# Down projection of a SwiGLU FFN: sixteen of its 22 blocks by seven products of halves

## The chip, the cores and the metric

The kernel runs on one core of one Trainium2 chip. The metric is the device time of one execution in microseconds, the median of several runs. The profile beside it comes from one further execution, taken by the hardware profiler. Engines are PE (TensorE), DVE (VectorE), ACT (ScalarE), POOL (GpSimd) and SP (SyncE, which here only issues DMAs).

## What is computed

One decoder layer on 512 tokens of width 1024 in float32: a norm, a projection, two attention-like head groups, an output projection with residual, and then the part that matters here, a dense FFN with `D_FF = 2816` and a last norm.

```python
def swiglu(x, w_gate, w_up, w_down):
    return (jax.nn.silu(x @ w_gate) * (x @ w_up)) @ w_down
...
        h = h + swiglu(rms_norm(h, norm_ffn[l]), w_gate[l], w_up[l], w_down[l])
    return rms_norm(h, norm_final)
```

The down projection is the last product, (512 x 2816) by (2816 x 1024), added to the residual.

## The kernel before

Every float32 matmul is made of three: each operand is split into a high part `hi` (a rounded copy, ACT, L144) and a low part `lo` (the rest, a subtraction on DVE, L146) by `split`, and `mm3` (L162 to L165) issues hi x hi, hi x lo and lo x hi into one PSUM bank. A matmul has a stationary operand of 128x128 and a moving one of 256 or 512 columns.

**FFN, gate and up** (L1174 to L1207). Eleven passes `q` make 256 of the 2816 hidden columns each. A pass forms gate and up from seven products of half-depth operands (`prod`, 24 matmuls of 256 columns each): the activations' sums and splits (`A11`, `S1`, ...) are made once and kept, in `gin` and `kB` among others, while `weight_side` loads four weight quarters, forms their sums (two by DMAs on POOL's queue that add into a tile, two on DVE) and splits seven operands `B11, B21, T2, T1, T3, B22, T4` into the rotating buffers `whi` and `wlo`, two of each. The results `hid` lie as [hidden column in block, token], four blocks of 128 to a `b8` tile and the last two in a `t4` tile.

**Down projection** (`accumulate`, called at L1211 with 22 blocks). Eight PSUM banks hold the whole output, four token tiles `t` by two halves `f` of the 1024 columns. For each pair of blocks, `weights` loads 256 rows of `w_down` (1 MB, SP's queue, three buffers `wraw`) and splits them into `whi`, `wlo` (in two halves); `jit` splits the hidden blocks into a ring in an `L` buffer. Then 48 matmuls of 128x512 follow, so 11 x 48 = 528 in all. The last four blocks run token tile by token tile, and behind each token tile come the residual, the final norm and the store.

Instructions stand in each engine's queue in an order that a scheduler chose when the program was built, by its own estimates and by priorities (`tc.high_priority`); on the chip every engine works down its queue in that order. Buffers are few: four of 16 KB a partition (`L`, one of them held by the residual `x2`), three `wraw`, two `whi`, two `wlo`, four `t4`. The PSUM banks are `s`, `pj`, `ra` (two each), `o` and `rb`.

Of the kernel before, what the change touches and what calls it, by code (L numbers as in the profile page):

```python
# [46 lines left out]
def hybrid_layer(ctx: ExitStack, tc: tile.TileContext, x, positions, norm_mix, w_in, mu_shift, w0, w2, a0, a2,  # L47
# [90 lines left out]


    def split(src, hi, lo, pool=False, lo_pool=False):  # L140
        if pool:
            POOL.tensor_copy(hi, src)
        else:
            ACT.activation(hi, src, AF.Copy)  # L144
        pool = pool or lo_pool
        (POOL if pool else DVE).tensor_sub(lo, src, hi.bitcast(F32))  # L146
# [1116 lines left out]
```

## Time and profile before

| | |
|---|---|
| median of 3 runs | 769.43 us (767.77 to 770.11) |
| the profiled execution's own time | 770.73 us |
| its span, first to last instruction | 769.0 us |
| first matmul of the down projection | 642.45 us |
| last matmul of the down projection | 761.93 us |
| mean granted PE clock over the span | 0.984 |

Times inside the span count from its first instruction. The span lies 1.7 us under the profiled execution's own time, which lies 1.3 us above the median. Busy time of an engine says how full its queue is, not that the others wait for it: that is read from the waits, and from the chain of work that ended last.

### The profile page before, as it was taken

The numbers are of one execution on the slowest core, as the hardware profiler recorded it, in microseconds if no ns is written. First come the engines' busy times: TensorE is split into PE (matmuls) and PEld (weight loads), VectorE is DVE, ScalarE is ACT, GpSimd is POOL, SyncE is SP. The second block draws the span as 40 slices with busy tenths as digits, with TensorE's granted clock in tenths as the row PEclk, the third lists the DMA queues.
The fourth block names the chain that finished last, engine by engine and source line by source line (L and its number), as shares of the span: only waits on it lengthen the run. The fifth ranks groups of instructions, "written<-read, shape, count | busy, mean of one in ns | idle before, by whom it ended". The sixth has DMA issues, their size and how long they took to land.

```text
span 769.0 us, 14989 instructions
## 1 busy us (share of the span) xinstructions
PE 738.6 (96%) x6093; PEld 648.1 (84%) x6093; DVE 543.3 (71%) x1052; ACT 381.5 (50%) x652; POOL 160.0 (21%) x258
## 2 busy tenths in 40 slices
PE   8999999998889999999996899999999999999996
PEld 7867888898877878867786899999999998888885
DVE  5488689789768987875659497888695994333235
ACT  7398643224277776676447344444443552233224
POOL 3210054058345542442001102020202000000000
PEclk9999999999989999999998999999999999999998
DMA  7722543100051000321218569696768444322102
GB/s 247 223 82 84 164 110 110 55 2 2 3 219 30 3 1 3 85 83 56 83 55 192 110 176 203 161 223 151 161 159 221 112 153 147 110 68 97 55 1 110
DMA packets 69243, 82.83 MB, mean 108 GB/s; under 512 B 4868, under 2 KB 62806, under 8 KB 69174
## 3 DMA queue, kind: packets, MB, share of 16 engines
q1 hardware_dynamic: 57558, 70.34, 28.5%
q0 software_dynamic: 11616, 11.54, 9.9%
q8 instruction: 48, 0.79, 0.4%
q14 instruction: 21, 0.17, 0.1%
HBM read 79.77 MB, written 2.10 MB: 106 GB/s over the span
## 4 chain that ended last, share of the span: by engine, by line
PE 74%; DVE 15%; DMA 6%; issue 2%; ACT 1%; POOL 0%; SPq 0%; DVEq 0%; POOLq 0%; ACTq 0%
PE ps_ra L165 7%; PE ps_ra L164 7%; PE ps_ra L163 6%; PE ps_pj L165 6%; PE ps_pj L163 6%; PE ps_pj L164 6%; PE ps_s L165 4%; PE ps_s L163 4%; PE ps_s L164 4%; PE ps_o L1001 3%; DVE wlo L146 3%; PE ps_pj L993 2%; DMA L<-in_w_up_dram 2%; DMA wraw<-in_w_up_dram 2%; DMA L<-in_w_gate_dram 2%
## 5 line engine op out<-in xcount | busy, mean ns | idle before, releaser
L144 ACT ACTIVATE whi<-wraw 128x1024 fp32r<-128x1024 f32 (+1 forms) x79 | 78.5, 1033 | 33.2 <-PE ps_s L165 8.2
L146 DVE TENSOR_TENSOR wlo<-wraw,whi 128x1024 fp32r<-128x1024 f32 (+1 forms) x62 | 77.7, 1284 | 14.9 <-ACT whi L144 11.3
L146 DVE TENSOR_TENSOR L<-b,L 128x512 fp32r<-128x512 f32 x24 | 16.2, 691 | 57.1 <-PE ps_rb L164 55.1
L990 POOL TENSOR_SCALAR whi<-whi,m,gates 128x128 f32<-128x128 f32 (+3 forms) x64 | 42.5, 679 | 36.9 <-DVE m L988 28.7
L144 ACT ACTIVATE L<-b 128x512 fp32r<-128x512 f32 x24 | 14.9, 632 | 70.0 <-PE ps_rb L164 65.1
L164 PE MATMUL ps_ra<-wlo,L 128*128 128x256 f32 (+1 forms) x140 | 47.6, 340 | 0.2 <-DVE wlo L146 0.2
L163 PE MATMUL ps_ra<-whi,L 128*128 128x256 f32 (+1 forms) x140 | 47.4, 340 | 0.2 <-ACT L L144 0.2
L165 PE MATMUL ps_ra<-whi,L 128*128 128x256 f32 (+1 forms) x140 | 47.0, 337 | 0.0
L165 PE MATMUL ps_pj<-whi,L 128*128 128x256 f32 (+1 forms) x140 | 46.3, 332 | 0.0
L164 PE MATMUL ps_pj<-wlo,L 128*128 128x256 f32 (+1 forms) x140 | 46.3, 331 | 0.0
L163 PE MATMUL ps_pj<-whi,L 128*128 128x256 f32 (+1 forms) x140 | 45.9, 332 | 0.0
L164 PE MATMUL ps_ra<-L,whi 128*128 128x256 f32 (+2 forms) x128 | 44.3, 346 | 1.0 <-DVE L L146 1.0
L163 PE MATMUL ps_ra<-L,whi 128*128 128x256 f32 (+2 forms) x128 | 44.1, 345 | 0.9 <-ACT L L144 0.9
L165 PE MATMUL ps_ra<-L,wlo 128*128 128x512 f32 (+2 forms) x120 | 41.2, 343 | 0.0
L987 ACT ACTIVATE whi<-whi,m 128x128 f32<-128x128 f32 (+3 forms) x64 | 35.4, 554 | 9.3 <-DVE m L986 8.1
L165 PE MATMUL ps_pj<-L,wlo 128*128 128x512 f32 (+1 forms) x112 | 38.8, 346 | 0.1
L163 PE MATMUL ps_pj<-L,whi 128*128 128x512 f32 (+1 forms) x104 | 36.3, 349 | 0.2 <-ACT whi L144 0.2
L164 PE MATMUL ps_pj<-L,whi 128*128 128x512 f32 (+1 forms) x104 | 35.9, 346 | 0.0
L986 DVE CUSTOM_DVE_ANT_0 whi<-ps_s,negb 128x128 f32<-128x128 f32 (+3 forms) x64 | 29.3, 484 | 5.9 <-PE ps_pj L993 2.5
L1137 POOL DMA_DIRECT2D t<-in_w_up_dram x6 | 7.9, 1322 | 115.1 <-DVE whi L146 50.4
L163 PEld LDWEIGHTS ps_ra<-whi,L 128*128 128x128 f32 x140 | 27.6, 197 | 3.1 <-ACT L L144 0.6
L164 PEld LDWEIGHTS ps_ra<-wlo,L 128*128 128x128 f32 x140 | 27.5, 196 | 3.0 <-DVE wlo L146 0.5
(627 smaller groups left out, 2462.4 us busy)
## 6 DMA issues: line engine op xcount, KB each, us to landing
wraw<-in_w_gate_dram SPq DMA_DIRECT2D x22, 512.0 KB
wraw<-in_w_down_dram SPq DMA_DIRECT2D x11, 1024.0 KB
wraw<-in_w_in_dram SPq DMA_DIRECT2D x9, 1024.0 KB
t<-in_w_up_dram POOLq DMA_DIRECT2D x12, 512.0 KB, 7.4
wraw<-in_w_up_dram SPq DMA_DIRECT2D x11, 512.0 KB
L<-in_w_up_dram POOLq DMA_DIRECT2D x10, 512.0 KB, 8.9
wraw<-in_w_out_dram SPq DMA_DIRECT2D x4, 1024.0 KB
wraw<-in_w_in_dram SPq DMA_DIRECT2D x6, 512.0 KB
```

Of the source, the lines that this page charges most:

```text
L144: ACT.activation(hi, src, AF.Copy)
L146: (POOL if pool else DVE).tensor_sub(lo, src, hi.bitcast(F32))
L163: PE.matmul(o, lh, rh, start=start, stop=False)
L164: PE.matmul(o, lh, rl, start=False, stop=False)
L165: PE.matmul(o, ll, rh, start=False, stop=stop)
L986: DVE.tensor_tensor_reduce(pr[:, i], pS[:, i], negb[:, S - n:S], scale=-1.0, scalar=3e38, op0=OP.add, op1=OP.min, accum_out=m[:, i, 0:1])
L987: ACT.activation(pr[:, i], pr[:, i], AF.Exp, scale=-1.0, bias=m[:, i, 0:1], accum_out=m[:, i, 1:2])
L990: POOL.tensor_scalar(pr[:, i], pr[:, i], m[:, i, 2:3], gv[:, 1 + b0 + i, h:h + 1], op0=OP.mult, op1=OP.mult)
L993: PE.transpose(pT[:, j], prr[:, x, j * 128:j * 128 + 128], ident)
L1001: PE.matmul(po[q, 2 * g:2 * g + 2], vtok[:, j % (t + 1), b0 + j // (t + 1), g], pTs[:, par, j], start=False, stop=g == 1 and bs[-1] == 1 a ...
L1137: POOL.dma_start(t1, quarter(w_up, 0), accum_op=OP.add)
```

## The change

The blocks 0 to 7 and 12 to 19 of the hidden dimension are paired into two groups, blocks 0 to 3 with 12 to 15 and 4 to 7 with 16 to 19 (`GROUPS`). A group is a product of a 2 x 2 arrangement of halves, tokens (0 to 255, 256 to 511) by blocks (first four, second four), with a 2 x 2 arrangement of weights, blocks by columns (0 to 511, 512 to 1023), and is formed from seven products `m1` to `m7` instead of eight. A product (`multiply`) is four blocks by two token tiles by `mm3`, 24 matmuls of 128x512 in two PSUM banks. The sums of activations are made in place on DVE (L1263, L1265, L1274, L1300), those of weights on DVE (L1269, L1271, L1298) and by DMAs on POOL's queue (L1270). `a_side` splits 1024 columns of activations into the rotating `whi` and `wlo`, `b_side` splits 2048 columns of weights, in two halves, into an `L` buffer, behind the last split of the FFN's weights (`issue_after`). First come `m1, m5, m6, m7` of the first group and of the second, then their sums go into the residual `x2` (L1277 to L1291), then `m2, m4, m3` of both groups. The remaining six blocks (`PLAIN`) run through `accumulate` as before, in the banks of `m2`, `m3`, `m4` and one more pair.

```diff
-    def accumulate(hi, lo, w, blocks, ahead=None):
-
-        banks = [ps(o) for o in ORDER]
+    def accumulate(hi, lo, w, blocks, ahead=None, rows=None, banks=None, empty=None):
+
+
+        rows = rows or [n * 256 for n in range(blocks // 2)]
+        banks = banks or [ps(o) for o in ORDER]
+        empty = empty or banks
...
+    GROUPS = ((0, 12), (4, 16))
+    PLAIN = (8, 9, 10, 11, 20, 21)
...
+    def a_side(v):
+        o = operand(("whi", "wlo")[turn2[0] % 2])
+        turn2[0] += 1
+        split(v, *o)
+        return o
+
+    def b_side(v):
+        o = st([128, 2, 4, 512], "L", dtype=F32R)
+        with tc.high_priority(), tc.issue_after(ends[0]), tc.issue_after(ends[1]):
+            for h in (slice(0, 2), slice(2, 4)):
+                split(v[h.start // 2] if type(v) is list else v[:, h], o[:, 0, h], o[:, 1, h])
+        return o[:, 0], o[:, 1]
...
+    def multiply(banks, a, b, first, last=False):
+        for i in range(4):
+            for t in range(2):
+                tl = slice(t * 128, t * 128 + 128)
+                mm3(banks[t], a[0][:, i, tl], a[1][:, i, tl], b[0][:, i], b[1][:, i], first and i == 0, last and i == 3)
...
+    m1, m5, m6, m7 = ([ps(o) for o in two] for two in (("o", "rb"), ("pj", "pj"), ("ra", "ra"), ("s", "s")))
+    t2s = []
+    for n, (a, b) in enumerate(GROUPS):
+        one, two = halves[n]
+        a11, a21, a12, a22 = (h[:, :, x] for h in (one, two) for x in (left, right))
+        first, last = n == 0, n == 1
+        t1, t2 = block4(a, 0, "wraw"), block4(b, 1, ("gin", "kB")[n])
+        t3 = st([128, 4, 512], "wraw") if first else None
+        t3 = [t3[:, 2 * i:2 * i + 2] if first else st([128, 2, 512], "t4") for i in range(2)]
+        for i in range(2):
+            nc.sync.dma_start(t3[i], down(a, 1)[:, 2 * i:2 * i + 2])
+        t2s.append(t2)
+        DVE.tensor_sub(a21, a22, a21)
+        multiply(m1, a_side(a11), b_side(t1), first, last)
+        DVE.tensor_add(a11, a21, a11)
+        with tc.high_priority():
+            for i in range(2):
+                h = slice(2 * i, 2 * i + 2)
+                DVE.tensor_add(t1[:, h], t1[:, h], t3[i])
+                POOL.dma_start(t3[i], down(b, 1)[:, h], accum_op=OP.add)
+            DVE.tensor_add(t2, t2, t1)
+        multiply(m5, a_side(a21), b_side(t1), first, last)
+        multiply(m6, a_side(a11), b_side(t2), first, last)
+        DVE.tensor_sub(a21, a11, a22)
+        multiply(m7, a_side(a21), b_side(t3), first, last)
+    u, w, v = (st([128, 2, 512], tag) for tag in ("t4", "t4", "t4"))
+    with tc.high_priority():
...
+        for t in range(2):
+            DVE.tensor_add(u[:, t], m1[t], u[:, t])
+            DVE.tensor_add(x2[:, t, lo_], m1[t], x2[:, t, lo_])
...
+    m2, m4, m3, rest = ([ps(o) for o in two] for two in (("o", "rb"), ("pj", "pj"), ("ra", "ra"), ("s", "s")))
+    for n, (a, b) in enumerate(GROUPS):
+        one, two = halves[n]
+        a11, a12, a22 = one[:, :, left], two[:, :, left], two[:, :, right]
+        b21, b22 = block4(b, 0, "wraw"), block4(b, 1, "wraw")
+        multiply(m2, a_side(a12), b_side(b21), n == 0)
+        DVE.tensor_add(t2s[n], t2s[n], b21)
+        multiply(m4, a_side(a22), b_side(t2s[n]), n == 0)
+        DVE.tensor_sub(a12, a12, a11)
+        multiply(m3, a_side(a12), b_side(b22), n == 0)
...
+    held = [m2[0], m3[0], m2[1], m3[1], m4[0], rest[0], m4[1], rest[1]]
+    for t, banks in accumulate(*jit(lambda k: hid[PLAIN[k]]), w_down, 6, None, [PLAIN[k] * 128 for k in (0, 2, 4)], held, rest):
```

Three places in the built order show where the new work stands. DVE's queue at the end of the FFN, before: `whi_7057` is the FFN's last operand (T4), the L1187 to L1207 rows evacuate the last products, and `wraw_7263` and `wraw_7323` are the first two loads of `w_down`.

```order
L146 TENSOR_TENSOR whi_7057<-t4_7028,whi_7057 128x1024
L1194 TENSOR_TENSOR t2_7062<-ps_ra_7143,t2_7060 128x512
L1197 TENSOR_TENSOR t2_7060<-ps_s_7169,t2_7060 128x512
L1198 TENSOR_TENSOR lora_7063<-ps_s_7169,t2_7062 128x512
L146 TENSOR_TENSOR wlo_7266<-wraw_7263,whi_7265 128x1024 x2
L1201 TENSOR_TENSOR t2_7062<-ps_pj_7196,t2_7062 128x512
L1202 SCALAR_TENSOR_TENSOR t4_7024<-t2_7062,t2_7061 128x2x256
L1205 TENSOR_TENSOR t2_7060<-ps_ra_7223,t2_7060 128x512
L146 TENSOR_TENSOR wlo_7326<-wraw_7323,whi_7325 128x1024 x2
L1207 SCALAR_TENSOR_TENSOR t4_7024<-lora_7063,t2_7060 128x2x256
```

The same queue after the change, from a little behind the same split on: `wraw_7259` is t1 and `gin_7261` t2 of the first group, `wlo_7267`, `whi_7305` are the activations of `m1` and `m5`, `L_7308` the weights of `m5`, and `b8_4804` the hidden blocks 0 to 3.

```order
L1269 TENSOR_TENSOR wraw_7259<-wraw_7259,wraw_7263 128x1024
L142 TENSOR_TENSOR wlo_7267<-b8_4804,wlo_7267 128x1024
L1199 TENSOR_TENSOR t2_7060<-ps_s_7169,t2_7060 128x512
L1200 TENSOR_TENSOR lora_7063<-ps_s_7169,t2_7062 128x512
L1269 TENSOR_TENSOR wraw_7259<-wraw_7259,wraw_7263 128x1024
L142 TENSOR_TENSOR whi_7305<-b8_4804,whi_7305 128x1024
L142 TENSOR_TENSOR L_7308<-wraw_7259,L_7308 128x1024
L1265 TENSOR_TENSOR b8_4804<-b8_4804 128x4x256
L1203 TENSOR_TENSOR t2_7062<-ps_pj_7196,t2_7062 128x512
L1271 TENSOR_TENSOR gin_7261<-gin_7261,wraw_7259 128x2048
L1207 TENSOR_TENSOR t2_7060<-ps_ra_7223,t2_7060 128x512
L142 TENSOR_TENSOR L_7308<-wraw_7259,L_7308 128x1024
```

The evacuations of the last FFN products, which stood nearly alone, now stand among sums and splits of the down projection. Further down DVE's queue before, within the down projection, there are two kinds of rows only, in turn:

```order
L146 TENSOR_TENSOR wlo_7386<-wraw_7383,whi_7385 128x1024 x2
L146 TENSOR_TENSOR L_7254<-b8_5220,L_7254 128x512 x2
L146 TENSOR_TENSOR wlo_7446<-wraw_7443,whi_7445 128x1024 x2
L146 TENSOR_TENSOR L_7254<-b8_5671,L_7254 128x512 x2
L146 TENSOR_TENSOR wlo_7506<-wraw_7503,whi_7505 128x1024 x2
```

After the change, DVE's queue at the point where the banks of `m1` (`ps_o_7251`, `ps_rb_7252`) are read out for the sums, so that `m2` can take them:

```order
L142 TENSOR_TENSOR L_7517<-t4_7407,L_7517 128x1024
L142 TENSOR_TENSOR L_7579<-wraw_7572,L_7579 128x1024 x2
L142 TENSOR_TENSOR whi_7609<-b8_6122,whi_7609 128x1024
L1298 TENSOR_TENSOR kB_7404<-kB_7404,wraw_7674 128x2048
L1283 TENSOR_TENSOR t4_7546<-ps_o_7251,t4_7546 128x512
L1284 TENSOR_TENSOR L_4391<-ps_o_7251,L_4391 128x512
L142 TENSOR_TENSOR L_7612<-gin_7261,L_7612 128x1024 x2
L1283 TENSOR_TENSOR t4_7546<-ps_rb_7252,t4_7546 128x512
L1284 TENSOR_TENSOR L_4391<-ps_rb_7252,L_4391 128x512
```

The readout of `o` stands behind the splits of `m2` and `m4`'s activations and behind a sum of 2048 columns. PE's queue before, where one bank of the down projection follows the other:

```order
L164 MATMUL ps_s_7256<-wlo_7446,L_7254 128x512
L165 MATMUL ps_s_7256<-whi_7445,L_7254 128x512
L163 MATMUL ps_s_7256<-whi_7445,L_7254 128x512
L164 MATMUL ps_s_7256<-wlo_7446,L_7254 128x512
L165 MATMUL ps_s_7256<-whi_7445,L_7254 128x512
```

PE's queue after, from the end of `m5` (`pj`) of the first group to the body of `m6` (`ra`); `s` is `m7`, and `o`, `rb` with `L_7414`, `wlo_7411` are `m1` of the second group:

```order
L160 MATMUL ps_pj_7254<-L_7308,whi_7305 128x512
L161 MATMUL ps_pj_7254<-L_7308,whi_7305 128x512
L162 MATMUL ps_pj_7254<-L_7308,whi_7305 128x512
L160 MATMUL ps_s_7257<-L_7373,whi_7370 128x512
L160 MATMUL ps_s_7258<-L_7373,whi_7370 128x512
L160 MATMUL ps_o_7251<-L_7414,wlo_7411 128x512
L160 MATMUL ps_rb_7252<-L_7414,wlo_7411 128x512
L161 MATMUL ps_ra_7255<-L_7340,wlo_7337 128x512
L162 MATMUL ps_ra_7255<-L_7340,wlo_7337 128x512
```

Two hi x hi matmuls each of `m7` and of the next group's `m1` stand ahead of the body of `m6`; in the order before, a bank's matmuls follow each other without any of a later product between them.

## Rows read from the trace of the kernel before

**Rows 1.** The page's part 1: busy time, share of the span and number of instructions of each engine.

```profile
PE 738.6 (96%) x6093; PEld 648.1 (84%) x6093; DVE 543.3 (71%) x1052; ACT 381.5 (50%) x652; POOL 160.0 (21%) x258
```

**Rows 2.** Stretches of 20 us: the stretch, its length, then busy us (and instructions) of PE, PEld, DVE, ACT and POOL, the granted PE clock, the share of the DMA engines and GB/s. The first lies in the FFN, the second in the down projection.

```profile
620.00:640.00 20.00, 20.00 (x170) 20.00 (x169) 16.44 (x19) 8.55 (x10) 0.00 (x0) 1.00 0.32 107
...
680.00:700.00 20.00, 20.00 (x90) 16.57 (x89) 6.80 (x8) 6.33 (x8) 0.00 (x0) 1.00 0.30 105
```

**Rows 3.** The chain that ended last, from 590 us on: start, us, what. The first matmul of the down projection, its last one, and the step behind it.

```profile
642.45 0.23 PE ps_s L163
...
761.93 0.24 PE ps_rb L165
762.19 0.70 DVE L L1230
```

**Rows 4.** Who waited for whom on PE between 440 and 769 us: us in total, times, longest. It is the only wait.

```profile
PE ps_ra L165 <- DVE wlo L146: 0.7, 1, 0.7
```

**Rows 5.** DVE in order of time within the down projection: start, us, line, what, count, and in brackets the idle time before it with its releaser.

```profile
653.15 1.37 DVE L146 TENSOR_TENSOR L<-b,L 128x512 fp32r<-128x512 f32 x2 [6.61 <-PE ps_rb L164]
654.78 2.36 DVE L146 TENSOR_TENSOR wlo<-wraw,whi 128x1024 fp32r<-128x1024 f32 x2 [0.26 <-ACT whi L144]
664.03 1.37 DVE L146 TENSOR_TENSOR L<-b,L 128x512 fp32r<-128x512 f32 x2 [6.89 <-PE ps_rb L164]
```

**Rows 6.** DVE in order of time in the FFN, four instructions in a row without idle time between them.

```profile
618.36 0.68 DVE L1197 TENSOR_TENSOR t<-ps_ra,t 128x512 f32<-128x512 f32 x1
618.96 0.68 DVE L1198 TENSOR_TENSOR smask<-ps_ra,t 128x512 f32<-128x512 f32 x1
619.56 1.21 DVE L146 TENSOR_TENSOR whi<-wraw,whi 128x1024 fp32r<-128x1024 f32 x1
620.69 1.21 DVE L146 TENSOR_TENSOR wlo<-wraw,wlo 128x1024 fp32r<-128x1024 f32 x1
```

**Rows 7.** ACT in order of time at the same place, two splits in a row, and the split of the last FFN operand.

```profile
617.38 1.05 ACT L144 ACTIVATE whi<-wraw 128x1024 fp32r<-128x1024 f32 x1
618.32 1.05 ACT L144 ACTIVATE wlo<-wraw 128x1024 fp32r<-128x1024 f32 x1
...
631.13 1.06 ACT L144 ACTIVATE whi<-t 128x1024 fp32r<-128x1024 f32 x1 [1.02 <-PE ps_pj L165]
```

**Rows 8.** DVE in order of time in the last pass of the FFN (q = 10): evacuations of products, and the last FFN weights' split (632.23).

```profile
631.08 0.69 DVE L1191 TENSOR_TENSOR t<-ps_pj,t 128x512 f32<-128x512 f32 x1 [0.48 <-PE ps_pj L165]
632.23 1.23 DVE L146 TENSOR_TENSOR whi<-t,whi 128x1024 fp32r<-128x1024 f32 x1 [0.47 <-ACT whi L144]
633.89 0.69 DVE L1194 TENSOR_TENSOR t<-ps_ra,t 128x512 f32<-128x512 f32 x1 [0.44 <-PE ps_ra L165]
636.76 0.69 DVE L1197 TENSOR_TENSOR t<-ps_s,t 128x512 f32<-128x512 f32 x1 [2.17 <-PE ps_s L165]
...
640.23 0.68 DVE L1201 TENSOR_TENSOR t<-ps_pj,t 128x512 f32<-128x512 f32 x1
...
642.49 0.69 DVE L1205 TENSOR_TENSOR t<-ps_ra,t 128x512 f32<-128x512 f32 x1 [0.85 <-PE ps_ra L165]
```

**Rows 9.** DVE in order of time earlier in the FFN: an idle stretch, and the four splits of the first down-projection blocks.

```profile
593.65 1.23 DVE L1141 TENSOR_TENSOR L<-L,wraw 128x1024 f32<-128x1024 f32 x1 [6.53 <-DMA L<-in_w_up_dram]
...
615.94 2.49 DVE L146 TENSOR_TENSOR L<-b,L 128x512 fp32r<-128x512 f32 x4
```

**Rows 10.** SP's queue in order of time, and stretches of 2 us behind its first issue (columns as in rows 2).

```profile
613.53 27.18 SPq L78 DMA_DIRECT2D wraw<-in_w_down_dram  x4
...
614.00:616.00 2.00, 2.00 (x19) 2.00 (x18) 1.90 (x4) 0.72 (x2) 0.00 (x0) 1.00 0.55 150
616.00:618.00 2.00, 2.00 (x19) 2.00 (x19) 2.00 (x4) 2.00 (x4) 0.00 (x0) 1.00 0.91 375
```

**Rows 11.** DMA issues: tile, queue, count, KB each, median us from issue to landing; then one such transfer as a piece of the chain that ended last.

```profile
t<-in_w_up_dram POOLq DMA_DIRECT2D x12, 512.0 KB, 7.4
...
L<-in_w_up_dram POOLq DMA_DIRECT2D x10, 512.0 KB, 8.9
...
583.96 9.67 DMA L<-in_w_up_dram
```

**Rows 12.** Stretches of 2 us at the seam of output projection and FFN (columns as in rows 2).

```profile
404.00:406.00 2.00, 0.69 (x7) 0.45 (x5) 2.00 (x3) 2.00 (x3) 0.00 (x0) 1.00 0.15 15
406.00:408.00 2.00, 1.30 (x9) 1.02 (x9) 2.00 (x3) 2.00 (x5) 0.00 (x0) 1.00 0.82 246
408.00:410.00 2.00, 0.47 (x2) 0.19 (x1) 2.00 (x3) 2.00 (x5) 0.97 (x1) 0.96 0.54 135
410.00:412.00 2.00, 1.55 (x7) 1.55 (x8) 2.00 (x4) 1.24 (x5) 0.34 (x1) 0.50 0.97 311
...
434.00:436.00 2.00, 1.97 (x17) 1.76 (x15) 0.00 (x0) 0.30 (x1) 0.00 (x0) 1.00 1.22 194
436.00:438.00 2.00, 0.00 (x0) 0.00 (x0) 1.92 (x2) 0.60 (x1) 0.00 (x0) 1.00 1.19 190
438.00:440.00 2.00, 1.51 (x12) 1.51 (x13) 2.00 (x3) 0.45 (x1) 0.00 (x0) 1.00 0.06 11
```

More of the change, by code (lines that the diff above doesn't have):

```diff
@@ L140, in split @@
     def split(src, hi, lo, pool=False, lo_pool=False):
[L141 to L146, printed above, removed]
+        a = POOL.tensor_copy(hi, src) if pool else ACT.activation(hi, src, AF.Copy)
+        b = (POOL if pool or lo_pool else DVE).tensor_sub(lo, src, hi.bitcast(F32))
+        return a.ins, b.ins
     def parts(raw, tags=("whi", "wlo"), pool=False, lo_pool=False):
@@ L1020, in run @@
                     wh, wl = (v[:, k % 2, f * 512:f * 512 + 512] for v in ws[k // 2])
-                    mm3(banks[t * 2 + f], a, b, wh, wl, k == 0, k == blocks - 1)
+                    o = banks[t * 2 + f]
+                    mm3(o, a, b, wh, wl, k == 0 and any(o is e for e in empty), k == blocks - 1)
         for n in range(blocks // 2):
-            ws[n] = weights(w[n * 256:n * 256 + 256], D)
+            ws[n] = weights(w[rows[n]:rows[n] + 256], D)
             if n < blocks // 2 - 2:
@@ L1104, in ffn_norm @@
             yield
-    turn2 = [0]
+    turn2, ends = [0], []
     def weight_side(q, b8=0):
@@ L1133, in put @@
                 turn2[0] += 1
-            split(v, *o[name])
+            ends[:] = split(v, *o[name])
         with tc.high_priority():
@@ L1172, in prod @@
         return o
-    hid = []
+    hid, hid4 = [], []
     for q in range(NF // 2):
@@ L1177, in hybrid_layer @@
             h4 = st([128, 4, S], "b8") if q < NF // 2 - 1 else st([128, 2, S], "t4")
+            hid4.append(h4)
         hq = h4[:, q % 2 * 2:q % 2 * 2 + 2]
@@ L1207, in hybrid_layer, with down @@
         DVE.scalar_tensor_tensor(hq[:, :, 256:512], u1, -1.0, u, op0=OP.mult, op1=OP.mult)
+    GROUPS = ((0, 12), (4, 16))
+    PLAIN = (8, 9, 10, 11, 20, 21)
+    halves = [(hid4[a // 4], hid4[b // 4]) for a, b in GROUPS]
+    lo_, hi_ = slice(0, 512), slice(512, 1024)
+    def down(row, f):
+        return w_down[row * 128:row * 128 + 512, f * 512:f * 512 + 512].rearrange("(k p) n -> p k n", p=128)
+    def a_side(v):
[3 more added lines that the diff above has]
+        return o
@@ new lines, in b_side, with block4 @@
+    def b_side(v):
[4 more added lines that the diff above has]
+        return o[:, 0], o[:, 1]
+    def block4(row, f, tag):
+        v = st([128, 4, 512], tag)
+        nc.sync.dma_start(v, down(row, f))
+        return v
+    def multiply(banks, a, b, first, last=False):
[3 more added lines that the diff above has]
+                mm3(banks[t], a[0][:, i, tl], a[1][:, i, tl], b[0][:, i], b[1][:, i], first and i == 0, last and i == 3)
@@ new lines, in hybrid_layer @@
+    u, w, v = (st([128, 2, 512], tag) for tag in ("t4", "t4", "t4"))
+    with tc.high_priority():
+        for t in range(2):
+            ACT.activation(w[:, t], m5[t], AF.Copy)
+        for t in range(2):
+            ACT.activation(u[:, t], m6[t], AF.Copy, scale=-1.0)
+        for t in range(2):
+            DVE.tensor_add(u[:, t], m1[t], u[:, t])
+            DVE.tensor_add(x2[:, t, lo_], m1[t], x2[:, t, lo_])
+        for t in range(2):
+            DVE.tensor_add(v[:, t], m7[t], u[:, t])
@@ new lines, in hybrid_layer @@
+    DVE.tensor_add(x2[:, 2:4, lo_], x2[:, 2:4, lo_], v)
+    DVE.tensor_add(v, v, w)
+    DVE.tensor_sub(x2[:, 2:4, hi_], x2[:, 2:4, hi_], v)
+    DVE.tensor_add(w, w, u)
+    DVE.tensor_sub(x2[:, 0:2, hi_], x2[:, 0:2, hi_], w)
+    m2, m4, m3, rest = ([ps(o) for o in two] for two in (("o", "rb"), ("pj", "pj"), ("ra", "ra"), ("s", "s")))
[8 more added lines that the diff above has]
+        multiply(m3, a_side(a12), b_side(b22), n == 0)
@@ L1210, in hybrid_layer @@
     o2 = st([128, 2, D], "b8")
-    for t, banks in accumulate(*jit(lambda k: hid[k]), w_down, NF):
+    held = [m2[0], m3[0], m2[1], m3[1], m4[0], rest[0], m4[1], rest[1]]
+    for t, banks in accumulate(*jit(lambda k: hid[PLAIN[k]]), w_down, 6, None, [PLAIN[k] * 128 for k in (0, 2, 4)], held, rest):
         xo, o = x2[:, t], o2[:, t % 2]
@@ L1224, in hybrid_layer @@
         ss = st([128, 4], "ss", 4)
-        lo_, hi_ = slice(0, 512), slice(512, 1024)
         DVE.tensor_add(xo[:, lo_], banks[0], xo[:, lo_])
```

1 line of the change is left out of this document (added).

## The prediction

> **What bounds the kernel now.** I read the busy shares first, then the waits, then the rows of the last 130 us. PE is busy for 96% of the span, DVE for 71%, ACT for 50% [rows 1]. From 440 us to the end PE shows a single wait, of 0.7 us [rows 4], and in the down projection PE is full at granted clock 1.00 while DVE works 6.8 of 20 us and ACT 6.3 [rows 2]. DVE there splits two 1024-column halves and two hidden blocks per pair of blocks and then idles for 6.89 us until PE gives buffers back [rows 5]. So this stage is bound by PE alone. Its 528 matmuls run from 642.45 to 762.17 (761.93 plus its piece of 0.24) [rows 3]: 119.72 / 528 = 0.2267 us each. About 7 us of norm and store follow, which the change leaves as they are. What this stage has to spare is DVE and ACT time, and the change spends it.
>
> **What is removed.** Sixteen blocks were 16 x 24 = 384 matmuls; fourteen products of 24 are 336. 48 matmuls of the same shape fall away: 48 x 0.2267 = 10.9 us, all on the path, if PE never waits for its operands. The whole stage is then 480 matmuls, 108.8 us, and could end at 642.45 + 108.8 = 751.3.
>
> **What is added on DVE.** Here lies the cost. Start to start, DVE takes 619.56 to 620.69 = 1.13 us for a 1024-column split and 618.36 to 618.96 = 0.60 us for 512 columns [rows 6]; the durations shown, 1.21 and 0.68, overlap with the next start. I take 1.135, since some neighbours lie at 1.14. A sum of 2048 columns is not in the trace: by the slope of the two it takes 1.135 + 2 x 0.53 = 2.20, as two of 1024 it takes 2.27; I take 2.20, since the slope comes from instructions of the same kind. In-place sums over runs of 256 columns (`128x4x256`) are not there either; bounds are 1.13 and the full duration of 1.22, and I take 1.13, the nearest row: as many columns, the same kind of operands.
>
> The last split of the FFN's weights starts on DVE at 632.23, held by PE (it waits for T2's buffer: ACT at 631.13 behind PE) [rows 7, 8]. That place does not move. From there the new order is one long queue. I add its rows up to three places.
>
> (a) To the second half of `m5`'s weights: 10 rows of 1024, 5 of 512 (evacuations of T1 to T4, which the order now mixes in), 1 of 2048: 11.4 + 3.0 + 2.2 = 16.6, done at 648.8. `m1`'s operands are done before 639, so PE starts `m1` at 642.45 as before and ends it at 647.9; `m5` needs its second half after another 12 matmuls, at 650.6. No wait. The late evacuations (T3's at about 638.5 against 636.76 in [rows 8], T4's at 647 against 642.49) hold nobody: `m1` uses `o` and `rb`, which are free, and `m5` and `m6` reach `pj` and `ra` behind them.
>
> (b) To the first half of the second group's `m5` weights: 17 more of 1024, 2 of 512, 1 of 2048: 19.3 + 1.2 + 2.2 = 22.7, done at 671.6. PE's side: `m5` and two matmuls of `m6` end at 653.8. Then come two of `m7` and two of the next `m1`, which stand ahead of `m6`'s body and wait for ACT. ACT splits every 0.94 us [rows 7], but it has stood still until PE freed `m1`'s activation buffer at 647.9; seven instructions later (about 654.4) `m7`'s activations are there, and one later (655.4) the first half of `m1`'s weights, whose `L` buffer PE gave back with `m5`. PE loses 0.7 + 0.5. From 655.9 it runs 66 matmuls, to 670.9, and waits for DVE until 671.6: 0.7 more.
>
> (c) To the readout of `o`, which `m2` waits for: 11 of 1024, 2 of 512, 2 of 2048: 12.5 + 1.2 + 4.4 = 18.1, done at 632.23 + 57.4 = 689.6. PE meanwhile waits 0.4 for `m6`'s first half (DVE 678.3), runs to 688.7 and waits 0.9.
>
> PE's waits are 1.2 + 0.7 + 0.4 + 0.9 = 3.2 us. At 689.6 it has 286 of the 480 matmuls ahead: 286 x 0.2267 = 64.9, end at 754.5. Behind that place the DVE rows for `m4`, `m3`, `m2`, `m4`, `m3` come 1 to 4 us ahead of PE's need, and the six plain blocks ask little of DVE, so nothing more is late. Net: 10.9 - 3.2 = **7.7 us less**.
>
> **ACT.** It makes the other half of each split at 0.94 us, under DVE's 1.13, and apart from the stretch in (b) it stays ahead of DVE. Its readouts of `m5` and `m6` stand where it has room. I cost it at nothing; DVE's longer queue is the cover.
>
> **What moves into the FFN.** Two sums of 1024 columns (L1263) come earlier. The first one stands just ahead of the row that DVE idled 6.53 us for [rows 9]: free. The second stands ahead of T3's split, where the removed 2.49 us of four hidden-block splits [rows 9] make more room than its 1.13. No FFN operand gets later.
>
> **Loads.** SP issues its first `w_down` load at 613.53 and the megabyte has moved by 618 [rows 10]; t1 takes that place, 19 us before its split. t3 and the second group's t1 follow as buffers come free (about 624 and 630), then t2 of the first group into `gin`, behind PE's last use of that operand at about 630.8. Even at the 190 GB/s of the seam [rows 12], the three megabytes issued from 624 to 630.8 are there by about 642, and t2 is asked for at 644.9. Behind the `gin` and `kB` loads on SP stand t3 of the second group and later `w_down` loads, none due before 650. POOL's adding transfers took 7.4 to 8.9 us and once 9.67 [rows 11]. Those of the first group go off at 637 and 641 and are wanted at 650 and 652: hidden. Those of the second go off at 668.2 and 669.3 and are wanted at about 677; with 9.67 they come 1.3 us late, of which 0.8 reaches the end.
>
> [...]
>
> **Rivals.**
> *PE alone sets the end.* If no wait appears, the gain is the whole 10.9: 758.5. For it speaks that PE is the only bound now; against it that the sums (b) and (c) leave DVE no idle time and still come last. 0.10.
> *DVE at full durations.* If each new DVE instruction takes its duration rather than its spacing, the queue is 38 x 1.22 + 9 x 0.68 + 4 x 2.4 = 62.1 instead of 57.4, the readout of `o` comes at 694.3, and 4.7 of the 7.7 us are gone: 766.4. Against it: rows in sequence never show that. It is also what other small delays in DVE's queue would sum to. 0.17. [...]
> *Slower: the PE clock falls.* Between 653 and 690 PE would now stop several times. [...] Against it: after 436 us PE had no matmul for 2 us and the clock stayed at 1.00 [rows 12], and no stop forecast here is over 1 us. [...] 0.06.
> *Late adding transfers* (POOL): the 0.8 us above, and as much again if two in a row queue up: about 763. 0.07.
> *The change does not do what it says:* the products are there in the order as written, 336 of them, so only a loss elsewhere, such as FFN operands late by several us, could bring it to zero. 0.04, near 769.
>
> **How the numbers follow.** Forecast: 769.43 - 7.7 = 761.7 against the median; the same step from the profiled execution's 770.73 would read 763.0. Its chance is 0.56, with about 1.5 us either way for the unknown 2048-column and strided sums (4 x 0.07 and 5 x 0.09 at most on the path). The range runs from PE alone, 758.5, to DVE at full durations, 766.5; outside lie the clock, the zero case and some of the DVE rival's upper part. What a measurement can tell from no change is 0.3%, 2.3 us. Faster by more: forecast, PE alone, late transfers and most of the DVE rival, 0.87; within: 0.07; slower: 0.06.
>
> **What would show it.** PE's matmuls of the stage should number 480 at 0.227 us and end at 754 to 755. DVE should show no idle time from 632 to about 700, with 1.13 us between 1024-column rows; the read of `o` (L1284) should start near 689. PE should wait about 0.7, 0.5, 0.7, 0.4 and 0.9 us in the places named, each for ACT or DVE, and not at all after 690; the granted clock should stay at 1.00. A DVE spacing over 1.15, idle time of DVE on a DMA, or a clock row under 1.00 between 650 and 690 would make the prediction wrong.

## The result

| | before | after |
|---|---|---|
| median, same chip | 769.77 us (767.77 to 770.28) | 762.56 us (762.07 to 762.75) |
| the profiled execution's own time | 770.73 us | 762.45 us |
| its span | 769.0 us | 760.6 us |
| matmuls of 128x512 in the stage | 528 | 480 |
| first of them starts | 642.28 us | 641.47 us |
| length of the stage | 119.7 us | 112.4 us |

The ratio is 0.991 [0.989, 0.993]: 7.2 us less between the medians, where 7.7 was forecast. "Stage" means here, in every kernel, the time from the start of the first to the end of the last 128x512 matmul in PE's order of time. Its start, 642.28 us before, is 0.17 ahead of the 642.45 of [rows 3], where the chain's piece of that matmul begins. It is the measure of the change: of the 8.4 us between the two spans 7.3 lie in it, 0.8 lie before its first matmul, and that start moved between 639.4 and 642.3 us over the kernels below, though the work ahead of the FFN is the same in all.

PE in order of time, kernel after: start, us, line, what, count, and in brackets the idle time before it with its releaser. The first and the last matmul of the stage, and every place where PE stopped.

```profile
641.47 0.40 PE L160 MATMUL ps_o<-L,wlo 128*128 128x512 f32 x1
...
652.60 0.39 PE L162 MATMUL ps_pj<-L,whi 128*128 128x512 f32 x1
653.57 0.73 PE L160 MATMUL ps_s<-L,whi 128*128 128x512 f32 x2 [0.58 <-ACT whi L141]
654.51 0.50 PE L160 MATMUL ps_o<-L,wlo 128*128 128x512 f32 x1 [0.21 <-ACT L L141]
...
670.10 0.61 PE L160 MATMUL ps_pj<-L,whi 128*128 128x512 f32 x2
670.81 0.50 PE L161 MATMUL ps_pj<-L,whi 128*128 128x512 f32 x1
...
673.23 0.61 PE L160 MATMUL ps_pj<-L,whi 128*128 128x512 f32 x2
674.10 0.72 PE L160 MATMUL ps_ra<-L,wlo 128*128 128x512 f32 x2 [0.26 <-ACT L L141]
...
687.66 0.61 PE L160 MATMUL ps_pj<-L,whi 128*128 128x512 f32 x2
688.90 0.50 PE L160 MATMUL ps_o<-L,wlo 128*128 128x512 f32 x1 [0.63 <-DVE L L1284]
...
753.64 0.39 PE L162 MATMUL ps_s<-whi,L 128*128 128x512 f32 x1
```

The durations overlap, so a stop is read from start to start. From 652.60 to 653.57 are 0.97 us for one matmul of 0.227: 0.74 lost, where the bracket has 0.58, since a row's 0.39 reaches 0.16 past the point at which the next could start. From 687.66 two matmuls should take until 688.11, the next starts at 688.90: 0.79 lost, and 0.11 at the one behind it. All such losses from 641.47 to 753.64 sum to 3.4 us, the forecast had 3.2. From 688.90 to the end there is none. [rows 4] had one wait of 0.7 us from 440 us on.

DVE in order of time, kernel after.

```profile
631.41 1.23 DVE L142 TENSOR_TENSOR whi<-t,whi 128x1024 fp32r<-128x1024 f32 x1 [0.46 <-ACT whi L141]
...
642.30 1.22 DVE L1265 TENSOR_TENSOR b<-b 128x1024 f32<-128x1024 f32 x1
643.43 0.68 DVE L1203 TENSOR_TENSOR t<-ps_pj,t 128x512 f32<-128x512 f32 x1
644.03 2.28 DVE L1271 TENSOR_TENSOR gin<-gin,wraw 128x2048 f32<-128x2048 f32 x1
646.24 0.68 DVE L1207 TENSOR_TENSOR t<-ps_ra,t 128x512 f32<-128x512 f32 x1
...
669.54 1.21 DVE L142 TENSOR_TENSOR L<-wraw,L 128x1024 fp32r<-128x1024 f32 x1
670.68 2.28 DVE L1271 TENSOR_TENSOR kB<-kB,wraw 128x2048 f32<-128x2048 f32 x1
...
687.57 0.68 DVE L1283 TENSOR_TENSOR t<-ps_o,t 128x512 f32<-128x512 f32 x1
688.17 0.68 DVE L1284 TENSOR_TENSOR L<-ps_o,L 128x512 f32<-128x512 f32 x1
...
700.76 1.23 DVE L142 TENSOR_TENSOR L<-wraw,L 128x1024 fp32r<-128x1024 f32 x1 [0.44 <-ACT L L141]
```

Where [rows 5] had gaps of 6.6 and 6.9 us, no bracket stands between the last FFN split (631.41) and 700.76. The 2048-column sum takes 644.03 to 646.24 = 2.21 us; the sum over runs of 256 columns takes 642.30 to 643.43 = 1.13, like any other row of 1024. The readout of `o` ends at 688.85, 57.4 us behind the start of the last FFN split: the forecast's own figure.

Stretches of 10 us, kernel after (columns as in [rows 2]).

```profile
650.00:660.00 10.00, 9.21 (x40) 6.96 (x39) 10.00 (x10) 6.36 (x8) 0.00 (x0) 1.00 0.47 163
...
680.00:690.00 10.00, 9.37 (x42) 7.45 (x41) 10.00 (x10) 6.11 (x9) 0.00 (x0) 1.00 0.33 105
690.00:700.00 10.00, 10.00 (x46) 8.27 (x45) 10.00 (x11) 2.21 (x3) 0.00 (x0) 1.00 0.27 83
```

The granted clock stays at 1.00 through the stops, and PE is full again from 690 on.

### The profile page after: what moved, and what is told of

Its sections match the earlier page's. It is cut to its first block, busy times and chain, and to the rows that moved or that the text cites. A ratio compares the mean times of both kernels' runs of the same rounds, so it can differ in the third digit from the quotient of the medians.

```text
span 760.6 us, 14951 instructions
## 1 busy us (share of the span) xinstructions
PE 726.7 (96%) x6045; PEld 636.6 (84%) x6045; DVE 593.4 (78%) x1089; ACT 399.5 (53%) x666; POOL 164.8 (22%) x262
## 4 chain that ended last, share of the span: by engine, by line
PE 74%; DVE 19%; issue 2%; DMA 2%; ACT 2%; POOL 0%; SPq 0%; DVEq 0%; ACTq 0%
PE ps_ra L161 7%; PE ps_ra L162 7%; PE ps_ra L160 7%; PE ps_pj L162 6%; PE ps_pj L160 6%; PE ps_pj L161 6%; PE ps_s L162 4%; PE ps_s L160 4%; PE ps_s L161 4%; PE ps_o L998 3%; DVE L L142 3%; DVE wlo L142 3%; PE ps_pj L990 3%; PE ps_s L977 1%; DVE t L554 1%
## 5 line engine op out<-in xcount | busy, mean ns | idle before, releaser
L141 ACT ACTIVATE whi<-wraw 128x1024 fp32r<-128x1024 f32 (+1 forms) x63 | 62.6, 1030 | 41.3 <-issue 13.5
L142 DVE TENSOR_TENSOR wlo<-wraw,whi 128x1024 fp32r<-128x1024 f32 (+1 forms) x46 | 58.8, 1305 | 16.6 <-ACT whi L141 13.1
L160 PE MATMUL ps_ra<-L,whi 128*128 128x512 f32 (+2 forms) x136 | 47.0, 347 | 1.4 <-ACT L L141 1.4
L161 PE MATMUL ps_ra<-L,whi 128*128 128x512 f32 (+2 forms) x136 | 47.2, 347 | 1.1 <-DVE L L142 1.1
L161 PE MATMUL ps_pj<-L,whi 128*128 128x512 f32 (+1 forms) x128 | 45.6, 356 | 0.1
L160 PE MATMUL ps_pj<-L,whi 128*128 128x512 f32 (+1 forms) x128 | 45.0, 358 | 0.0
L160 PE MATMUL ps_ra<-whi,L 128*128 128x256 f32 (+1 forms) x108 | 34.8, 324 | 0.5 <-ACT L L141 0.5
L161 PE MATMUL ps_ra<-wlo,L 128*128 128x256 f32 (+1 forms) x108 | 34.9, 323 | 0.2 <-DVE wlo L142 0.2
L162 PE MATMUL ps_ra<-whi,L 128*128 128x256 f32 (+1 forms) x108 | 34.3, 320 | 0.0
L162 PE MATMUL ps_pj<-whi,L 128*128 128x256 f32 (+1 forms) x108 | 33.9, 315 | 0.0
L160 PE MATMUL ps_pj<-whi,L 128*128 128x256 f32 (+1 forms) x108 | 33.6, 315 | 0.0
L162 PEld LDWEIGHTS ps_ra<-L,wlo 128*128 128x128 f32 (+1 forms) x144 | 27.1, 188 | 4.2 <-issue 0.5
L161 PEld LDWEIGHTS ps_ra<-L,whi 128*128 128x128 f32 (+1 forms) x136 | 25.7, 189 | 4.8 <-DVE L L142 1.3
L160 PEld LDWEIGHTS ps_ra<-L,whi 128*128 128x128 f32 (+1 forms) x136 | 25.7, 189 | 4.7 <-ACT L L141 1.6
L161 PEld LDWEIGHTS ps_pj<-L,whi 128*128 128x128 f32 x128 | 25.0, 195 | 3.5 <-DVE L L142 0.5
```

The source lines that it names most:

```text
L141: a = POOL.tensor_copy(hi, src) if pool else ACT.activation(hi, src, AF.Copy)
L142: b = (POOL if pool or lo_pool else DVE).tensor_sub(lo, src, hi.bitcast(F32))
```

## The experiments

**Theory A** is the prediction's: one queue on DVE, from the FFN's last split to the readout of `o`, with no idle time in it, sets when PE's operands and banks are ready; whatever makes it shorter or starts it earlier ends PE's waits. (The forecast's first wait, 1.2 us at the first `m7` and the next `m1`, stands outside of it: it was priced on ACT.) **Theory B**: the waits are the price of handing over between products (ACT's splits, the readouts, the matmuls of a later product ahead of an earlier one's body) and don't hang on DVE's sums.

In each ratio the kernel before ran on the same chip, at a median of 769.77, 769.52 (e1 to e4) or 769.26 us (the others).

| run | median us | ratio to before | stage us | lost |
|---|---|---|---|---|
| after | 762.56 | 0.9910 [0.9891, 0.9929] | 112.4 | 3.4 |
| e5_no_sums | 756.86 | 0.9840 [0.9820, 0.9860] | 108.8 | 0 |
| e3_no_issue_after | 757.94 | 0.9853 [0.9837, 0.9869] | 109.7 | 0.8 |
| e10_free_order_and_read | 759.34 | 0.9866 [0.9846, 0.9887] | 109.1 | 0.2 |
| e2_dve_late | 763.08 | 0.9913 [0.9897, 0.9929] | 112.4 | 3.4 |
| e6_one_group | 766.21 | 0.9958 [0.9945, 0.9971] | 117.0 | 2.7 |
| e4_sums_on_pool | 766.55 | 0.9965 [0.9952, 0.9977] | 116.9 | 8.0 |
| e1_dve_early | 768.70 | 0.9996 [0.9985, 1.0006] | 119.8 | 10.9 |
| e9_lo_twice | 771.20 | 1.0030 [1.0017, 1.0043] | 122.6 | 13.6 |

"Lost" sums what each step from one 128x512 matmul to the next takes beyond 0.227 us, where that is more than 0.06.

**No sums.** All of DVE's sums of activations and weights are left out, so the seven products are made of other operands; the matmuls, splits and loads stay.

```diff
-        DVE.tensor_sub(a21, a22, a21)
...
-        DVE.tensor_add(a11, a21, a11)
-                DVE.tensor_add(t1[:, h], t1[:, h], t3[i])
-            DVE.tensor_add(t2, t2, t1)
-        DVE.tensor_sub(a21, a11, a22)
...
-        DVE.tensor_add(t2s[n], t2s[n], b21)
-        DVE.tensor_sub(a12, a12, a11)
```

> The changed kernel with all sums of activations and of weights on DVE (L1263, L1265, L1269, L1271, L1274, L1298, L1300) left out, so what it computes is not the reference's; the 480 matmuls, the splits, the loads and POOL's transfers stay. The stage from the first to the last 128x512 matmul took 112.4 us in the changed kernel, 108.8 of it matmuls. Theory A (DVE's queue makes the waits): 108.8 to 109.5, the end about 3 us earlier. Theory B (buffers given back, ACT, the two hoisted matmuls): 111.5 to 112.4.

PE shows no wait, and the stage is 108.8 us, the bare 480 x 0.2267. In number that is Theory A's forecast. But PE's order changed with the edit. PE in order of time, this kernel:

```profile
650.12 0.39 PE L162 MATMUL ps_pj<-L,whi 128*128 128x512 f32 x1
650.35 0.39 PE L160 MATMUL ps_ra<-L,wlo 128*128 128x512 f32 x1
```

`m5` is followed at once by `m6`, and `m6` runs whole: none of the four matmuls of `m7` and of the next `m1` that stand ahead of its body in the kernel after is left there. So this run shows that the 3.4 us go with the sums. It doesn't separate DVE's time from the matmuls ahead of another product's body, which Theory B blames and which went too.

**No issue_after.** `b_side`'s splits may stand anywhere in the queue.

```diff
-        with tc.high_priority(), tc.issue_after(ends[0]), tc.issue_after(ends[1]):
+        with tc.high_priority():
```

> The changed kernel without issue_after in b_side; in the built order the two splits of m1's weights move ahead of the FFN's splits T1, T3, B22 and T4 on DVE. Theory A: DVE had about 1.3 us of idle time just ahead of the T4 split, PE's FFN operands still come in time, and what moved ahead leaves the queue behind it, so 1.0 to 1.3 us less: 761.4. Rival (the wait is needed): FFN operands come late and PE stops in the FFN, 763.5 to 765.

DVE in order of time, this kernel, and PE's only stop.

```profile
615.43 2.35 DVE L142 TENSOR_TENSOR L<-wraw,L 128x1024 fp32r<-128x1024 f32 x2
...
628.64 1.21 DVE L1269 TENSOR_TENSOR wraw<-wraw 128x1024 f32<-128x1024 f32 x1
...
631.51 1.22 DVE L142 TENSOR_TENSOR whi<-t,whi 128x1024 fp32r<-128x1024 f32 x1
...
683.73 0.67 DVE L1284 TENSOR_TENSOR L<-ps_o,L 128x512 f32<-128x512 f32 x1
```

```profile
683.32 0.61 PE L160 MATMUL ps_pj<-L,whi 128*128 128x512 f32 x2
684.46 0.50 PE L160 MATMUL ps_o<-L,wlo 128*128 128x512 f32 x1 [0.52 <-DVE L L1284]
```

The two weight splits of `m1` now stand at 615.43, in room that DVE had in the FFN, and the split of the last FFN operand (631.51) has no idle time ahead of it. The two sums L1269, which overwrite t1 in place and so come behind those splits, moved ahead of it too (628.64 and 630.38). Four rows, 4.5 us, have left the queue behind the last FFN split, and that split stands 1.8 us later against the stage's start: 2.7 us net. From the first 128x512 matmul (639.77) to the end of the readout (684.40) are 44.6 us, against 47.4 in the kernel after: 2.75 less, and the stage is 2.75 shorter. The expectation had the direction and too small a size: with the earlier splits the waits for ACT at `m7`, `m1` and `m6` went too. PE's order changed there too (`m6`'s body now stands ahead of the next `m1`'s first two matmuls), so the gain is that of the earlier rows and of the order that the scheduler made of them. FFN operands are not late: PE is busy for 40.00 of the 40 us from 600 to 640.

**Another readout, on top of that.** ACT copies `m1`, so that DVE reads each bank of `m1` once instead of twice.

```diff
-            ACT.activation(u[:, t], m6[t], AF.Copy, scale=-1.0)
+            ACT.activation(u[:, t], m1[t], AF.Copy)
+            DVE.tensor_add(x2[:, t, lo_], m1[t], x2[:, t, lo_])
         for t in range(2):
-            DVE.tensor_add(u[:, t], m1[t], u[:, t])
-            DVE.tensor_add(x2[:, t, lo_], m1[t], x2[:, t, lo_])
+            DVE.tensor_sub(u[:, t], u[:, t], m6[t])
```

> Without issue_after, and with m1's readout made simpler: ACT copies m1 where it copied m6, DVE adds m1 to the residual and subtracts m6 from the copy, so that one DVE row less stands ahead of the release of o. The kernel without issue_after alone had a stage of 109.65 with one wait of 0.79 us on that readout. Theory A: the wait falls by about 0.6, a stage of 109.0, about 757.3. Rival (the wait has another cause, such as ACT's readout of m6): 109.65.

```profile
685.47 0.61 PE L160 MATMUL ps_pj<-L,whi 128*128 128x512 f32 x2
686.00 0.50 PE L160 MATMUL ps_o<-L,wlo 128*128 128x512 f32 x1
```

PE's order of time at the same place: the next matmul of `o` starts 0.08 us late instead of 0.69. The stage is 109.1 us, as expected, 0.2 above the bare matmuls. Up to this place PE's 194 matmuls stand in the same order in both kernels, and against the stage's start the readout of `o` ends 0.61 us sooner (44.02 us behind it, not 44.63). The rival, ACT's readout of `m6`, was not the brake before either: DVE's two rows on `o` (from 683.13 in the run before) follow the row ahead of them without idle time. So it was one row less on DVE that took 0.61 us off the wait. The median is not lower than that of the run before it (757.51 to 761.77 against 757.34 to 758.91): in the profile its stage starts at 641.92 instead of 639.77, ahead of anything the edit touches. Which of the two is the faster kernel stays open; both beat the kernel after.

**DVE work behind the readout.** Four more rows of 1024 columns on DVE behind the sums into `x2` (`max` of a tile with itself).

```diff
     DVE.tensor_sub(x2[:, 0:2, hi_], x2[:, 0:2, hi_], w)
+    for _ in range(4):
+        DVE.tensor_tensor(x2[:, 0:2, hi_], x2[:, 0:2, hi_], x2[:, 0:2, hi_], op=OP.max)
```

> The changed kernel with four more 1024-column DVE instructions (4.5 us) on the residual behind the last of the sums (maximum with itself), that is after 713 us. Theory A: DVE is ahead of PE there (plain blocks ask little of it), so 762.6, at most 0.5 more. A theory in which any DVE work of this stage counts: 767.

The stage and each stop are those of the kernel after, and PE's order is the same. The four rows ran at 719 to 728 us, 30 us behind the readout; DVE's time costs nothing there.

**DVE work ahead of it.** Two more rows of 2048 columns behind the first group's t2.

```diff
             DVE.tensor_add(t2, t2, t1)
+            for _ in range(2 if first else 0):
+                DVE.tensor_tensor(t2, t2, t2, op=OP.max)
```

> The changed kernel with two more 2048-column DVE instructions behind the first group's t2 sum (each takes the maximum of t2 with itself, so values stay). Theory A (DVE's queue from the last FFN split to the readout of m1 is what PE waits for): the readout of o comes 2 x 2.2 = 4.4 us later and the end with it, about 767.0 against 762.6 of the changed kernel, so 2.8 us under the kernel before. Theory B (PE's waits come from ACT and from buffers given back, DVE is only busy beside it): 763.0 or less, since DVE's extra work fits its own slack.

Slower, but not in the way expected. The readout of `o` moved back by 4.6 us against the stage's start, near the expected 4.4, but PE did not wait there. PE's order changed (`m5` now runs whole), the scheduler set the two rows apart, and t2 was whole only at 657.5. In order of time, DVE, ACT and PE of this kernel, and the stretch around it:

```profile
655.19 2.28 DVE L1273 TENSOR_TENSOR gin<-gin 128x2048 f32<-128x2048 f32 x1
```

```profile
657.51 1.06 ACT L141 ACTIVATE L<-gin 128x1024 fp32r<-128x1024 f32 x1 [5.68 <-DVE gin L1273]
```

```profile
658.62 1.22 PE L160 MATMUL ps_ra<-L,wlo 128*128 128x512 f32 x2 [7.94 <-ACT L L141]
```

```profile
650.00:654.00 4.00, 0.67 (x3) 0.21 (x2) 4.00 (x4) 1.06 (x1) 0.00 (x0) 1.00 0.13 50
654.00:656.00 2.00, 0.00 (x0) 0.00 (x0) 2.00 (x3) 0.00 (x0) 0.00 (x0) 0.56 0.00 0
656.00:664.00 8.00, 5.38 (x13) 3.97 (x14) 8.00 (x7) 5.79 (x6) 0.00 (x0) 0.50 0.00 1
```

PE stood for 8.1 us at two matmuls of `m6` that have nothing to do with the readout, and behind them the clock was at 0.50: the next 13 matmuls took 2.9 us more than at 0.227 each. So this run shows that a row on DVE ahead of an operand can stop PE, but its size is that of another wait than the one forecast, with these 2.9 us on top.

**The lower parts twice.** The second group's four activation splits make their `lo` half twice, 4 x 1.13 us.

```diff
-    def a_side(v):
+    def a_side(v, twice=False):
...
+        if twice:
+            DVE.tensor_sub(o[1], v, o[0].bitcast(F32))
...
-        multiply(m1, a_side(a11), b_side(t1), first, last)
+        multiply(m1, a_side(a11, last), b_side(t1), first, last)
```

(and so for `m5`, `m6`, `m7`).

> The changed kernel with the low part of the second group's four activation operands of the first loop made twice (the same subtraction into the same place, values stay). In the built order three of the four extra rows of 1.135 us stand ahead of the readout of o, spread among the other rows. Theory A: the readout and the end 3.4 us later, a stage of 115.8 against 112.4, about 766. Theory B: under 113.

```profile
685.63 0.73 PE L160 MATMUL ps_pj<-L,whi 128*128 128x512 f32 x2 [1.15 <-ACT L L141]
691.24 0.80 PE L160 MATMUL ps_o<-L,wlo 128*128 128x512 f32 x1 [4.87 <-DVE L L1286]
691.83 0.63 PE L161 MATMUL ps_o<-L,wlo 128*128 128x512 f32 x1
692.26 0.63 PE L162 MATMUL ps_o<-L,wlo 128*128 128x512 f32 x1
```

PE in order of time at `m2` (L1286 is here what L1284 was, two lines having been added). The readout moved back by 3.4 us against the stage's start, as expected; the stage grew by 10.2, far more than that. The built order tells the rest: 20 matmuls of `m7` (bank `s`) that PE ran ahead of `o` in the kernel after now stand behind it, so that PE had 20 x 0.227 = 4.5 us less to do while it waited. The first of the two places, the kernel after's rows with a minus, this kernel's with a plus:

```
-L161 MATMUL ps_s<-L,whi 128x512
-L162 MATMUL ps_s<-L,whi 128x512
...
-L162 MATMUL ps_s<-L,whi 128x512
-L160 MATMUL ps_s<-L,whi 128x512 x2
+L161 MATMUL ps_s<-L,whi 128x512 x2
```

Behind the wait of 4.87 us the rows show 0.43 us from matmul to matmul (691.83 to 692.26) where 0.227 is usual; ten such steps and the first one behind the stop (0.59) cost 2.2 us more than in the kernel after. The granted clock stood at 0.50 there, from 689.3 to 696.2 us. 3.4 + 4.5 + 2.2 = 10.1 of the 10.2.

**One group.** Only blocks 0 to 3 with 12 to 15 by seven products, 14 plain blocks (504 matmuls).

```diff
-    GROUPS = ((0, 12), (4, 16))
-    PLAIN = (8, 9, 10, 11, 20, 21)
+    GROUPS = ((0, 12),)
+    PLAIN = (4, 5, 6, 7, 8, 9, 10, 11, 16, 17, 18, 19, 20, 21)
...
```

> Half of the change: only the first group (8 of the 22 blocks) by seven products, 14 blocks as before, so 504 matmuls, 114.3 us. Theory A: the first group's own waits stay (0.74 + 0.49 + 0.11 behind m5), those that DVE's longer queue of the second group made go, so a stage of about 115.7 against 119.7 before and 112.4, about 765.5. If the waits came with each group in equal parts: 116.0. If the seven products cost something else each time (a fixed price of the readouts): 117 or more.

Half of the matmuls are saved (24, 5.4 us) and 2.7 of the 3.4 us are still lost. PE in order of time:

```profile
653.66 0.73 PE L160 MATMUL ps_s<-L,whi 128*128 128x512 f32 x2 [0.58 <-ACT whi L141]
...
665.24 0.73 PE L160 MATMUL ps_pj<-L,whi 128*128 128x512 f32 x2 [0.81 <-ACT L L141]
666.43 0.51 PE L160 MATMUL ps_o<-L,wlo 128*128 128x512 f32 x1 [0.45 <-DVE L L1284]
```

The first stop (at `m7`) and the last (at `m2`'s bank `o`) are those of the kernel after, only sooner; the middle one, at `m4`'s first two matmuls, is new. `m2` to `m4` now follow sooner, and ACT could make the split that these two need only behind DVE's 2048-column sum for `m4`'s weights (661.76 to 664.04); PE starts them 1.20 us behind the end of that sum. So the stage is longer than expected, and the losses are not shared out by groups: the way into the products and the way to `m2` cost something with one group already. At 117.0 us it is as long as the expectation's last theory had it, a fixed price of the readouts. The rows don't bear that out: of the 2.7 us 0.85 lie at `m7`, 1.1 behind the sum for `m4`, and 0.7 at the readout. The second group then takes 4.6 us off the stage (117.0 to 112.4), of the 5.4 that its saved matmuls are worth.

**The second group's sums on POOL.**

```diff
-        DVE.tensor_add(a11, a21, a11)
+        (POOL if last else DVE).tensor_add(a11, a21, a11)
...
-        DVE.tensor_sub(a21, a11, a22)
+        (POOL if last else DVE).tensor_sub(a21, a11, a22)
...
-        DVE.tensor_sub(a12, a12, a11)
+        POOL.tensor_sub(a12, a12, a11)
```

> The changed kernel with four activation sums on POOL (second group's two in the first loop, both of the second loop). Theory A: three 1024-column rows, 3.4 us, leave DVE's queue ahead of the readout of o, and of PE's 3.4 us of waits the 2.05 that DVE causes go; the 1.3 us at the hoisted matmuls stay: 760.5. Theory B: 762.6. Rival: POOL (a 1024-column sum takes 2.4 to 3.0 us there) delivers late or slows DVE down while both run: 763 or more.

The expectation failed: the stage is 4.5 us longer, not shorter. POOL and DVE in order of time, this kernel:

```profile
652.13 15.18 POOL L1265 TENSOR_TENSOR b<-b 128x1024 f32<-128x1024 f32 x1 [10.43 <-DVE wlo L142]
667.39 2.40 POOL L1274 TENSOR_TENSOR b<-b,b 128x1024 f32<-128x1024 f32 x1
...
678.84 6.73 POOL L1300 TENSOR_TENSOR b<-b,b 128x1024 f32<-128x1024 f32 x1 [5.17 <-DVE wlo L142]
```

```profile
663.85 1.22 DVE L1269 TENSOR_TENSOR wraw<-wraw,t 128x1024 f32<-128x1024 f32 x1
668.44 2.43 DVE L142 TENSOR_TENSOR wlo<-b,wlo 128x1024 fp32r<-128x1024 f32 x1 [3.37 <-ACT wlo L141]
...
682.08 1.21 DVE L142 TENSOR_TENSOR L<-t,L 128x1024 fp32r<-128x1024 f32 x1
683.98 2.67 DVE L142 TENSOR_TENSOR L<-wraw,L 128x1024 fp32r<-128x1024 f32 x1 [0.69 <-ACT L L141]
```

POOL's row of 652.13 ends at 667.31, 2.24 us behind the end of DVE's last row ahead of its gap (665.07); that of 678.84 ends at 685.57, 2.28 behind DVE's row of 682.08. Both seem to have begun only when DVE paused, and then to take what the row of 667.39 takes, begun while DVE stood, 2.40. The other way round, DVE's rows of 668.44 and 683.98 both end 1.08 us behind POOL's. The splits of `m5`'s activations waited for POOL, PE for them (1.79 and 2.0 us at `m5`), and the clock went to 0.50 behind that:

```profile
674.00:680.00 6.00, 5.67 (x13) 4.46 (x14) 6.00 (x6) 3.53 (x5) 1.16 (x1) 0.50 0.84 159
```

The 13 matmuls from 674.33 on took 2.8 us more than at 0.227 each. DVE's queue became shorter, but the sums came later.

## Why the prediction was right

**What is removed** was right to the row: 480 matmuls, and 0.227 us each where PE does not wait (108.8 us without sums).

**DVE's queue** was right in its sum and in its rows: 57.4 us forecast and measured, spacing 1.13 to 1.14, 2.21 for the 2048-column sum (2.20 taken), 1.13 for the strided one. The rival of full durations (766.4) falls by that. The trace shows that the spacing, not the duration, is what a queue without gaps pays: the rows last 1.21 to 1.23 us and start 1.13 to 1.14 apart.

**PE's waits** were right in sum and mixed in their parts:

| place | forecast | measured |
|---|---|---|
| first `m7` and next `m1`, on ACT | 1.2 | 0.74 + 0.49 + 0.11 |
| second `m5`, on DVE | 0.7 | 0.26 + 0.11 |
| second `m6`'s first two matmuls, on ACT | none | 0.42 + 0.12 |
| second `m6`'s body | 0.4 | 0.13 + 0.11 |
| `m2`, on the readout of `o` | 0.9 | 0.79 + 0.11 |
| sum | 3.2 | 3.4 (with rounding) |

DVE finished the awaited half of `m5`'s weights at 670.75, 39.3 us behind the last FFN split, as forecast (39.4). The wait was half as long because I had the whole product wait for it: the two hi x hi matmuls at 670.10 need ACT's part alone, and ran first. The wait that I did not see has the same cause the other way round. Two matmuls of `m6` stand inside `m5`'s body and need the high half of t2's second-group copy, which ACT can make only behind DVE's 2048-column sum (670.68 to 672.96):

```profile
672.99 1.06 ACT L141 ACTIVATE L<-kB 128x1024 fp32r<-128x1024 f32 x1 [0.68 <-DVE kB L1271]
...
676.23 1.07 ACT L141 ACTIVATE L<-t 128x1024 fp32r<-128x1024 f32 x1 [0.28 <-DMA t<-in_w_down_dram]
```

ACT in order of time, kernel after. I had priced the same pattern at the first group and left it out at the second; "ACT at nothing" was off by these 0.5 us, ACT's 1.06 us behind DVE's sum. `m5` and the body of `m6` came out 0.3 and 0.2 us under the forecast, this wait 0.5 over it. That these errors cancel in the sum is luck; the waits at `m7` and at `m2` were right by themselves.

What the first of these waits is made of stands in ACT's rows. ACT in order of time, kernel after:

```profile
647.19 1.06 ACT L141 ACTIVATE wlo<-b 128x1024 fp32r<-128x1024 f32 x1 [2.50 <-PE ps_rb L162]
...
652.47 1.04 ACT L141 ACTIVATE whi<-b 128x1024 fp32r<-128x1024 f32 x1
```

ACT stood until PE gave the activation buffer back, then worked without a gap and delivered `m7`'s activations at 653.51, 0.06 us ahead of PE's start. The forecast had it so (647.9 and 654.4). DVE's queue has no part in these 1.3 us.

**That the queue is the cause** holds for 2.05 of the 3.4 us, the waits at the second group's `m5` and `m6` and at `m2`: each ends within 0.1 us of a DVE row, or of the ACT row that DVE's sum released, and up to there DVE has no gap. For the wait at `m2` it is also shown by an edit, since one row less ahead of the readout took 0.61 us off it with PE's order unchanged. The runs without sums and with the earlier splits fit this, but changed PE's order too. The other 1.3 us, at the first `m7` and the next `m1`, are ACT's, as forecast, which is what Theory B says of them. They stand unchanged in the runs that keep PE's order there (sums on POOL, lower parts twice) and are gone in those that change it (no sums, and both without issue_after); whether the order or the earlier splits took them away is not shown.

**Loads and the adding transfers.** The second row above is the only trace of them: ACT waited 0.28 us for t3 of the second group, and nothing of it reached PE. The rival of late transfers (763) did not come true.

**What moves into the FFN.** PE is busy for 30.00 of the 30 us from 612 to 642, to the end of the FFN; no operand came late.

**The clock.** It stayed at 1.00 through stops of 0.2 to 0.8 us. The rival was real nonetheless: in three of the runs, at stops of 3.8 us (in two parts), 5.2 and 8.1 us, the granted clock fell to 0.50, and the 11 to 13 matmuls behind them took 2.4 to 2.9 us more than at 0.227 each.

**The size.** 7.3 us came out of the stage (7.7 forecast from 112.05 against 112.4 measured: 0.2 in waits, the rest in steps a hundredth or two over 0.227). Ahead of it the two profiles differ by 0.8 us, which the change does not explain and which the start's scatter covers.

## What to carry to other kernels

When PE work is bought with work of another engine, add up that engine's queue by start-to-start spacing, from the last place where it is held back to each place that PE waits for; the sum was good to 0.1 us in 57, while busy shares (DVE 78% after) say nothing of it. Then walk PE's order and ask for each matmul that stands ahead of its product's body which half of which operand it needs; that is where the parts went wrong. And look first for idle time of the same engine upstream: letting two splits go early, into room in the FFN, and with them the two sums that had to come behind them, was worth 2.75 us more than the order that held them back (with the order of PE that came of it).
